# Inverse roots by token: their Newton steps on GpSimd instead of VectorE

## The chip, the cores and the metric

The kernel runs on 1 core of one Trainium2 chip. The metric is the device time of one execution in microseconds (us); lower is better. Before the change it is 2480.51 us, the median of 3 runs (2478.15 to 2484.81).

The engines carry the profile's names: PE (TensorE), DVE (VectorE), ACT (ScalarE), POOL (GpSimd), and SP, which issues most of the DMAs. PSUM is the memory that PE writes its results to, SBUF the working memory of all engines.

## What is computed

Two layers of an encoder trunk for 544 tokens (512 of a prompt and 32 of a sample, which share the weights), model width 1024. Each sub-layer is fed by an RMSNorm and its output is normed again before it is added to the residual h:

```python
def rmsnorm(x, g):
    y = xf * lax.rsqrt(jnp.mean(xf * xf, axis=-1, keepdims=True) + EPS)
    return (y * g.astype(jnp.float32)).astype(x.dtype)

def layer(h, p, ...):
    h = h + FFN_RES * rmsnorm(swiglu(rmsnorm(h, g_ff1_pre), w_ff1_gu, w_ff1_down), g_ff1_post)
    m, state = token_mix(rmsnorm(h, g_mix_pre), ...)          # three kinds of attention
    h = h + rmsnorm(m, g_mix_post)
    h = h + FFN_RES * rmsnorm(swiglu(rmsnorm(h, g_ff2_pre), w_ff2_gu, w_ff2_down), g_ff2_post)
    gate = jax.nn.sigmoid(rmsnorm(h, g_ple_pre) @ w_ple_gate)
    h = h + rmsnorm((p @ w_ple_proj) * gate, g_ple_post)
```

What matters here is the factor `rsqrt(mean(x*x) + EPS)`, one number for each token.

## The kernel before

**Layout.** Activations lie with the feature on the partition and the token on the free axis: h is eight tiles of 128 features by 544 tokens. The tokens are worked in two halves (HALVES): the first has 256 columns, the second 288. Every fp32 operand of a matrix product is split in a high and a low part (`split`, L111: ACT copies the high part, DVE subtracts it from the source, which is recorded as L109 and L113), and `gemm` (L233) makes three matmuls of each block, L238 to L240. A weight block of 128x1024 thus costs a DMA, an ACT copy and a DVE subtraction before PE can use it. The weights arrive through two buffers `raw`.

**The norm by halves.** `Normed` (L245) holds the input of a sub-layer without its root: `chunk` (L255) multiplies h by the gain and splits it (xa, xb; L258, L259) and `square` sums the squares (L205 on ACT, L211 on DVE). The products are made from that, and the root multiplies their result: `up` in `ffn` does `tt(g, pg, x.r(c0, c1))` (L346, L348), `job` in `ple` does it in L973. So PE can run ahead of the root until all six PSUM banks that such products use hold a result that waits for it (three called acc, two prj, one pv). `Finish` (L279) ends a sub-layer: `scale` (L289) makes the root of the output y, `fill` (L297) runs over eight chunks of a half, on DVE z = y * gain * root (L303) and h = h + z (L304), and hands each to the next sub-layer's `chunk`.

**Two ways to the root.** `rstd_wide` (L193) works on the whole 128 x 256 or 128 x 288 tile with Ln and Exp on ACT; the mix (attention) and its entry use it, and the change leaves it alone. `rstd` (L155) works by token: PE adds the squares over the partitions with a matmul against ones (L165, L167), so that the sums of 128 (or 96) tokens stand on as many partitions in 2 (or 3) columns. DVE turns them into v (L171) and a first guess by integer arithmetic (L172, L173), and then runs three Newton steps on the 128x2 or 96x3 tile, three instructions each:

```python
            for _ in range(3):
                tt(e, rc, rc, op=ALU.mult)
                tt(e, e, v, op=ALU.mult)
                stt(rc, e, 1.5, rc, op0=ALU.add, op1=ALU.mult)
```

These are L175, L176 and L177. PE then spreads the root over all partitions with matmuls against the identity (L179, into a tile called tr), and either ACT copies it to SBUF (`copy`, recorded as L109 r<-tr) or DVE reads it from PSUM (L303 with an input tr). `rstd` is called 20 times. Ten places call it, once for each half: the input of the first ffn; in layer 0 the input of the second ffn, its output, the input of ple, the output of ple and the input of the next layer's first ffn; in layer 1 the input of the second ffn, its output, and ple's input and output. In the text they are sites 0 to 19 in order of time, two for each place: sites 2 and 3 (and 12 and 13 in layer 1) are the input of the second ffn, sites 8 and 9 the output of ple in layer 0, 10 and 11 the input of the next ffn, 18 and 19 the output of ple at the program's end.

**What sets the order.** The program is written in the order of the computation, but each engine's instruction order is made by a list scheduler that runs over the whole program with its own estimates of durations and with priorities (`tc.high_priority(300)` around `rstd`). Engines then run their queues strictly in that order and wait on semaphores. A change to one engine's work therefore moves instructions on the others too. DVE's queue mixes the Newton instructions with the fill's and the weight splits; PE's queue holds L179 at the place at which the scheduler expects the root.

POOL has little to do in the kernel: it clears tiles, copies 32x32 blocks (L687) and issues some DMAs, nearly all in the mix.

Of the kernel before, what the change touches and what calls it, by code (L numbers as in the profile page):

```python
# [12 lines left out]
ALU = mybir.AluOpType  # L13
# [22 lines left out]
def trunk(ctx: ExitStack, tc, a, outs, depth=2):  # L36
    nc = tc.nc
# [19 lines left out]
    def tl(tag, shape, dt=F32):  # L57
        count[0] += 1
        tag = alias.get(tag, tag)
        p, n = where[tag]  # L60
        return p.tile(shape, dt, tag=tag, name=f"{tag}_{count[0]}", bufs=n)
# [40 lines left out]
    tt = nc.vector.tensor_tensor  # L102
    stt = nc.vector.scalar_tensor_tensor
# [4 lines left out]
    def copy(out, in_):  # L108
        act(out, in_, AF.Copy)  # L109
# [32 lines left out]
    def load_gains(l):  # L142
# [9 lines left out]
        bfs.append(at.pop("b_f")[0])  # L152
        gains.append(at)

    def rstd(out, acc, n, last=None, rc=None):  # L155


        w = acc.shape[1]
        m = 128 if w % 128 == 0 else 96
        k = w // m  # L160
        with tc.high_priority(300):
            t = bank("tr")
            for i in range(k):
                to, c = t[0:m, 288 + 2 * i:290 + 2 * i], slice(i * m, i * m + m)
                mm(to, acc[:, c], ones[:, 0:2], start=True, stop=last is None)  # L165
                if last is not None:
                    mm(to, last[:, c], ones[:, 0:2], start=False, stop=True)  # L167
            sums = t[0:m, 288:288 + 2 * k].rearrange("p (t two) -> p t two", two=2)[:, :, 0]
            v, e = tl("n", [128, 4])[0:m, 0:k], tl("n", [128, 4])[0:m, 0:k]
            rc = (tl("n", [128, 4]) if rc is None else rc)[0:m, 0:k]  # L170
            ts(v, sums, -0.5 / n, -0.5 * EPS, op0=ALU.mult, op1=ALU.add)  # L171
            ts(rc.bitcast(I32), v.bitcast(I32), 1, MASK, op0=ALU.arith_shift_right, op1=ALU.bitwise_and)  # L172
            ts(rc.bitcast(I32), rc.bitcast(I32), -1, MAGIC, op0=ALU.mult, op1=ALU.add)  # L173
            for _ in range(3):
                tt(e, rc, rc, op=ALU.mult)  # L175
                tt(e, e, v, op=ALU.mult)  # L176
                stt(rc, e, 1.5, rc, op0=ALU.add, op1=ALU.mult)  # L177
            for i in range(k):
                mm(t[:, i * m:i * m + m], rc[:, i:i + 1].to_broadcast([m, 128]), ident[0:m, 0:m], start=True, stop=True)  # L179
            if out is None:  # L180
                return t[:, 0:w]
            copy(out, t[:, 0:w])
# [62 lines left out]
    class Normed:  # L245
# [23 lines left out]
        def r(s, c0, c1):  # L269
            if c0 not in s.done:  # L270
                s.done.add(c0)
                i = c0 // 128
                if s.wide:
                    rstd_wide(s.R[:, c0:c1], s.acc[:, c0:c1], D, tmp="q")
                    return s.R[:, c0:c1]
                rstd(s.R[:, c0:c1], s.acc[:, c0:c1], D, s.last.get(c0), s.rc[:, i:i + 4])
            return s.R[:, c0:c1]

    class Finish:  # L279
# [9 lines left out]
        def scale(s, cols):  # L289
            c0, c1 = cols  # L290
            acc = s.R[c0] = s.acc[:, c0:c1]
            if s.wide:
                rstd_wide(acc, acc, D)
            else:
                s.R[c0] = rstd(None, acc, D, s.last.get(c0))
# [816 lines left out]
def build(nc, shapes, depth=2):  # L1112
    from concourse import mybir as _m
    import numpy as np
    args = {k: nc.dram_tensor(f"in_{k}_dram", s, _m.dt.float32, kind="ExternalInput").ap() for k, s in shapes.items()}
    outs = [nc.dram_tensor(f"out_{i}_dram", s, _m.dt.float32, kind="ExternalOutput").ap()
            for i, s in enumerate(_outputs(depth))]
    with tile.TileContext(nc, schedule_with_timeline_sim=True) as tc:
        trunk(tc, args, outs, depth)
    return len(outs)  # L1120
# [13 lines left out]
```

## Time and profile before

| | |
|---|---|
| median of 3 runs | 2480.51 us |
| profiled execution, its own time | 2481.84 us |
| its span, first to last instruction | 2480.0 us |
| PE busy (matmuls) | 2390.8 us, 96% |
| DVE busy | 1443.3 us, 58% |
| ACT busy | 1083.7 us, 44% |
| POOL busy | 71.7 us, 3% |
| TensorE clock granted, mean | 0.981 |

Durations are read from the one profiled execution. A wait is time in which an engine's next instruction was held back, and it is put down to the instruction that released it. Times in a timeline count from the start of the span.

### The profile page before, as it was taken

What the parts mean: (1) busy time and instruction counts of PE and PEld (TensorE: products, weight loads), DVE (VectorE), ACT (ScalarE), POOL (GpSimd) and SP (SyncE); (2) the same over time, 40 slices, a digit from 0 to 9 for tenths busy, and PEclk for the clock granted to TensorE, in tenths of its full rate; (3) what the DMA queues carried; (4) which work ended last, traced back from release to release, by engine and by line L of the source; (5) the groups of instructions that cost most, each with busy time, mean ns of one, the idle gap of its engine ahead of it and who ended that gap; (6) DMA issues with size and microseconds to landing.
All of it is one profiled execution on the core that took longest, in us unless ns stands there. A gap on an engine that the chain in (4) does not pass through costs nothing.

```text
span 2480.0 us, 45319 instructions
## 1 busy us (share of the span) xinstructions
PE 2390.8 (96%) x18342; PEld 2302.4 (93%) x18342; DVE 1443.3 (58%) x3236; ACT 1083.7 (44%) x2347; POOL 71.7 (3%) x244
## 2 busy tenths in 40 slices
PE   9999999999998999999999999999999989999997
PEld 8999999987788999999999999999876889999997
DVE  6344446777857344446863444477777573444466
ACT  5322224668854322224533222246788543222343
POOL 0000000211000000000000000001110000000000
PEclk9999999999998999999999999999999999999998
DMA  5323322322023323322213323232311233323221
GB/s 161 108 79 90 100 66 82 95 89 55 27 65 115 111 80 90 99 86 86 82 47 98 98 72 106 56 97 91 101 33 34 77 111 98 95 74 102 85 69 37
DMA packets 73600, 207.44 MB, mean 84 GB/s; under 512 B 9312, under 2 KB 18152, under 8 KB 73392
## 3 DMA queue, kind: packets, MB, share of 16 engines
q1 hardware_dynamic: 70288, 195.93, 26.5%
q0 software_dynamic: 3104, 8.62, 1.1%
q8 instruction: 144, 2.36, 0.4%
q14 instruction: 64, 0.52, 0.1%
HBM read 188.21 MB, written 11.85 MB: 81 GB/s over the span
## 4 chain that ended last, share of the span: by engine, by line
PE 88%; DVE 6%; ACT 3%; DMA 2%; issue 1%; SPq 0%; DVEq 0%; ACTq 0%
PE acc L238 12%; PE acc L239 12%; PE acc L240 12%; PE prj L238 10%; PE prj L239 10%; PE prj L240 10%; PE pv L238 4%; PE pv L239 4%; PE pv L240 4%; PE acc L405 2%; PE tr L135 1%; DMA raw<-in_w_ff_gu_dram 1%; DVE z L303 1%; PE pv L427 1%; PE pv L429 1%; PE pv L428 1%
## 5 line engine op out<-in xcount | busy, mean ns | idle before, releaser
L109 ACT ACTIVATE wx<-raw 128x1024 fp32r<-128x1024 f32 (+3 forms) x149 | 139.3, 936 | 269.8 <-PE acc L239 99.4
L109 ACT ACTIVATE wh<-raw 128x1024 fp32r<-128x1024 f32 (+3 forms) x157 | 151.2, 966 | 228.9 <-PE acc L239 101.9
L113 DVE TENSOR_TENSOR wl<-raw,wh 128x1024 fp32r<-128x1024 f32 (+3 forms) x157 | 173.6, 1107 | 80.8 <-ACT wh L109 80.0
L109 ACT ACTIVATE m<-q 128x256 fp32r<-128x256 f32 (+1 forms) x224 | 94.9, 428 | 256.9 <-DVE q L349 251.9
L113 DVE TENSOR_TENSOR wx<-raw,wx 128x1024 fp32r<-128x1024 f32 (+3 forms) x149 | 159.4, 1070 | 77.8 <-ACT wx L109 75.8
L238 PE MATMUL prj<-xa,wh 128*128 128x256 f32 (+3 forms) x632 | 186.4, 295 | 4.6 <-DVE q L346 2.7
L239 PE MATMUL prj<-xb,wh 128*128 128x256 f32 (+3 forms) x632 | 186.2, 295 | 4.5 <-DVE xb L259 4.5
L240 PE MATMUL prj<-xa,wl 128*128 128x256 f32 (+3 forms) x632 | 184.5, 292 | 0.0
L238 PE MATMUL acc<-xa,wx 128*128 128x256 f32 (+1 forms) x600 | 173.9, 290 | 5.4 <-ACT wx L109 5.4
L240 PE MATMUL acc<-xa,wx 128*128 128x256 f32 (+1 forms) x600 | 173.9, 290 | 0.0
L239 PE MATMUL acc<-xb,wx 128*128 128x256 f32 (+1 forms) x600 | 173.6, 289 | 0.0
L239 PE MATMUL acc<-xb,wh 128*128 128x288 f32 (+1 forms) x576 | 166.7, 290 | 0.0
L240 PE MATMUL acc<-xa,wl 128*128 128x288 f32 (+1 forms) x576 | 166.5, 290 | 0.0
L238 PE MATMUL acc<-xa,wh 128*128 128x288 f32 (+1 forms) x576 | 165.6, 290 | 0.0
L240 PE MATMUL prj<-xa,wx 128*128 128x288 f32 (+1 forms) x480 | 139.8, 291 | 1.3 <-DVE wx L113 1.3
L238 PE MATMUL prj<-xa,wx 128*128 128x288 f32 (+1 forms) x480 | 140.4, 293 | 0.0
L239 PE MATMUL prj<-xb,wx 128*128 128x288 f32 (+1 forms) x480 | 140.3, 292 | 0.0
L347 ACT ACTIVATE q<-q 128x256 f32<-128x256 f32 (+1 forms) x176 | 74.3, 425 | 145.6 <-DVE q L346 141.2
L239 PEld LDWEIGHTS prj<-xb,wh 128*128 128x128 f32 (+1 forms) x632 | 119.6, 189 | 7.1 <-DVE xb L259 6.2
L238 PEld LDWEIGHTS prj<-xa,wh 128*128 128x128 f32 (+1 forms) x632 | 119.4, 189 | 7.3 <-DVE q L346 3.2
L240 PE MATMUL acc<-xa,wy 128*128 128x288 f32 (+1 forms) x424 | 123.4, 291 | 0.8 <-DVE wy L113 0.8
L238 PE MATMUL acc<-xa,wy 128*128 128x288 f32 (+1 forms) x424 | 123.7, 292 | 0.4 <-ACT wy L109 0.4
(525 smaller groups left out, 8128.2 us busy)
## 6 DMA issues: line engine op xcount, KB each, us to landing
raw<-in_w_ff_gu_dram SPq DMA_DIRECT2D x174, 512.0 KB, 3.6
raw<-in_w_ff_down_dram SPq DMA_DIRECT2D x64, 384.0 KB, 3.2
raw<-in_w_ff_down_dram SPq DMA_DIRECT2D x64, 320.0 KB, 2.9
raw<-in_w_in_dram SPq DMA_DIRECT2D x22, 512.0 KB, 3.5
raw<-in_w_out_dram SPq DMA_DIRECT2D x16, 512.0 KB, 3.6
raw<-in_w_ple_gate_dram SPq DMA_DIRECT2D x16, 512.0 KB, 3.5
raw<-in_w_v_dram SPq DMA_DIRECT2D x8, 512.0 KB, 3.6
xb<-r SPq DMA_DIRECT2D x32, 128.0 KB, 2.3
```

Of the source, the lines that this page charges most:

```text
L109: act(out, in_, AF.Copy)
L113: tt(lo, src, f(hi), op=ALU.subtract)
L135: nc.tensor.transpose(out, in_, ident[0:n, 0:n])
L238: mm(p, wh[k], xh[k][:, c0:c1], start=i == 0, stop=False)
L239: mm(p, wh[k], xl[k][:, c0:c1], start=False, stop=False)
L240: mm(p, wl[k], xh[k][:, c0:c1], start=False, stop=i == len(ks) - 1)
L303: stt(t, s.y[c][:, c0:c1], s.g[c], s.R[c0], op0=ALU.mult, op1=ALU.mult)
L347: act(g, g, AF.Silu)
L405: one = mm(ss[e][:, 0:w], z[a_][:, qs], z[b_][:, 0:w], start=(a_, b_) == (0, 2), stop=False)
L427: mm(Oe, vh, ph[:, j, :], start=e == 0 and j == 0, stop=False, skip_group_check=True)
L428: mm(Oe, vl, ph[:, j, :], start=False, stop=False, skip_group_check=True)
L429: mm(Oe, vh, pl[:, j, :], start=False, stop=j == 2 * b + 1, skip_group_check=True)
```

## The change

The three-instruction Newton step goes from DVE to POOL, where it takes four instructions, since the fused add and multiply is split in two. v, the integer guess, the matmuls and the copies stay where they are, and so does `rstd_wide`.

```diff
+    ptt, pts = nc.gpsimd.tensor_tensor, nc.gpsimd.tensor_scalar
+
     def rstd(out, acc, n, last=None, rc=None):
...
             ts(rc.bitcast(I32), v.bitcast(I32), 1, MASK, op0=ALU.arith_shift_right, op1=ALU.bitwise_and)
             ts(rc.bitcast(I32), rc.bitcast(I32), -1, MAGIC, op0=ALU.mult, op1=ALU.add)
             for _ in range(3):
-                tt(e, rc, rc, op=ALU.mult)
-                tt(e, e, v, op=ALU.mult)
-                stt(rc, e, 1.5, rc, op0=ALU.add, op1=ALU.mult)
+                ptt(e, rc, rc, op=ALU.mult)
+                ptt(e, e, v, op=ALU.mult)
+                pts(e, e, 1.5, None, op0=ALU.add)
+                ptt(rc, rc, e, op=ALU.mult)
             for i in range(k):
                 mm(t[:, i * m:i * m + m], rc[:, i:i + 1].to_broadcast([m, 128]), ident[0:m, 0:m], start=True, stop=True)
```

The lines behind it move down by three: L179 is L182 in the changed kernel, L303 is L306, L346 is L349. In the program, 180 instructions leave DVE's queue and 240 enter POOL's, and the scheduler orders the queues anew; PE and ACT have as many instructions as before.

POOL's queue at its head, in the changed kernel (n is the tile of v or e, rc that of the root; ISA is an instruction that the compiler puts in):

```order
L397 MEMSET pa_5189 128x128
L397 MEMSET pa_5190 128x128
L177 ISA
L177 TENSOR_TENSOR n_300<-rc_124 128x2
L178 TENSOR_TENSOR n_300<-n_300,n_299 128x2
L179 TENSOR_SCALAR n_300<-n_300 128x2
L180 TENSOR_TENSOR rc_124<-rc_124,n_300 128x2
L177 TENSOR_TENSOR n_300<-rc_124 128x2
```

Site 0's chain stands right behind the first two clears, with an ISA row ahead of it that stands nowhere else in front of such a chain; each link but the first waits for the one before it.

PE's queue at site 2, the input of the second ffn of layer 0 (acc, prj and pv are the six banks, wh and wl a weight's two parts), before:

```order
L238 MATMUL acc_9408<-xa_9035,wh_9401 128x256
L239 MATMUL acc_9408<-xb_9043,wh_9401 128x256
L240 MATMUL acc_9408<-xa_9035,wl_9402 128x256
L179 MATMUL tr_9293<-cst,rc_9046 128x128 x2
L238 MATMUL prj_9479<-xa_9028,wh_9467 128x256
```

and in the changed kernel:

```order
L241 MATMUL acc_9417<-xa_9038,wh_9410 128x256
L242 MATMUL acc_9417<-xb_9046,wh_9410 128x256
L182 MATMUL tr_9299<-cst,rc_9052 128x128 x2
L243 MATMUL acc_9417<-xa_9038,wl_9411 128x256
L241 MATMUL acc_9417<-xa_9039,wh_9410 128x256
L242 MATMUL acc_9417<-xb_9047,wh_9410 128x256
```

The spreading matmuls have moved up by ten matmuls, from behind the sixth bank's last product into the middle of that product. Behind them the first product that needs a freed bank is prj, in both.

DVE's queue at the same site, where the root is first used (L346 and L348, in the changed kernel L349 and L351), before:

```order
L211 TENSOR_TENSOR r_9044<-r_9044,z_9170 128x288
L304 TENSOR_TENSOR y_8734<-t_9175,z_9173 128x288
L177 SCALAR_TENSOR_TENSOR rc_9046<-n_9299,rc_9046 128x2
L303 SCALAR_TENSOR_TENSOR z_9183<-y_8770,gt_77,r_8500 128x288
L259 SCALAR_TENSOR_TENSOR xb_9040<-y_8734,gt_77,xa_9032 128x288
L304 TENSOR_TENSOR y_8770<-t_9185,z_9183 128x288
L211 TENSOR_TENSOR r_9044<-r_9044,z_9180 128x288
L303 SCALAR_TENSOR_TENSOR z_9193<-y_8806,gt_77,r_8500 128x288
L346 TENSOR_TENSOR q_9291<-prj_9241,r_9045 128x256
L348 TENSOR_TENSOR q_9292<-pv_9242,r_9045 128x256
```

and in the changed kernel:

```order
L214 TENSOR_TENSOR r_9050<-r_9050,z_9156 128x288
L307 TENSOR_TENSOR y_8639<-t_9161,z_9159 128x288
L113 TENSOR_TENSOR wx_9483<-raw_9480,wx_9482 128x1024
L349 TENSOR_TENSOR q_9297<-prj_9247,r_9051 128x256
L351 TENSOR_TENSOR q_9298<-pv_9248,r_9051 128x256
L349 TENSOR_TENSOR q_9394<-acc_9344,r_9051 128x256
L306 SCALAR_TENSOR_TENSOR z_9169<-y_8704,gt_77,r_8506 128x288
```

The use of the root has moved up past two chunks of the fill and one weight split: it stands behind the fill's third chunk and the split of the fourth weight.

## Rows read from the trace of the kernel before

**Rows 1.** The page: busy time, then the chain that ended last.
```profile
PE 2390.8 (96%) x18342; PEld 2302.4 (93%) x18342; DVE 1443.3 (58%) x3236; ACT 1083.7 (44%) x2347; POOL 71.7 (3%) x244
PE 88%; DVE 6%; ACT 3%; DMA 2%; issue 1%; SPq 0%; DVEq 0%; ACTq 0%
```

**Rows 2.** Waits of PE: waiting line, releaser, us in total, times, longest.
```profile
PE tr L179 <- DVE rc L177: 17.3, 3, 7.3
PE tr L179 <- DVE n L177: 3.0, 2, 2.4
```

**Rows 3.** Stretches: length, busy us (count) by engine, PEclk, DMA share, GB/s.
```profile
755.00:790.00 35.00, 26.39 (x193) 25.89 (x193) 29.06 (x79) 17.59 (x34) 0.00 (x0) 0.80 0.31 97
790.00:1145.00 355.00, 355.00 (x2834) 355.00 (x2833) 161.94 (x280) 107.65 (x178) 0.00 (x0) 1.00 0.31 92
```

**Rows 4.** Timeline of PE at sites 2, 12, 10, 19: start, us, instruction [idle before].
```profile
764.18 0.28 PE L240 MATMUL acc<-xa,wl 128*128 128x256 f32 x1
771.73 1.22 PE L179 MATMUL tr<-cst,rc 128*128 128x128 f32 x4 [7.28 <-DVE rc L177]
774.28 0.58 PE L238 MATMUL prj<-xa,wh 128*128 128x256 f32 x1 [1.33 <-DVE q L346]
...
775.09 0.41 PE L238 MATMUL prj<-xa,wh 128*128 128x256 f32 x1
775.30 0.41 PE L239 MATMUL prj<-xb,wh 128*128 128x256 f32 x1
...
2005.51 0.58 PE L238 MATMUL prj<-xa,wh 128*128 128x256 f32 x1 [1.32 <-DVE q L346]
...
1256.81 0.71 PE L179 MATMUL tr<-cst,rc 128*128 128x128 f32 x4 [3.08 <-DVE rc L177]
...
2468.69 1.59 PE L179 MATMUL tr<-cst,n 96*128 96x96 f32 x6 [2.38 <-DVE n L177]
```

**Rows 5.** Timeline of DVE at site 2, from the guess to the root's use.
```profile
757.66 0.16 DVE L173 TENSOR_SCALAR rc<-rc 128x2 int32<-128x2 int32 x1
758.15 0.15 DVE L175 TENSOR_TENSOR n<-rc 128x2 f32<-128x2 f32 x1
758.84 1.23 DVE L113 TENSOR_TENSOR wl<-raw,wh 128x1024 fp32r<-128x1024 f32 x1 [0.53 <-ACT wh L109]
759.98 0.94 DVE L303 SCALAR_TENSOR_TENSOR z<-y,gt,r 128x288 f32<-128x288 f32 x2
...
765.84 1.23 DVE L113 TENSOR_TENSOR wx<-raw,wx 128x1024 fp32r<-128x1024 f32 x1 [0.73 <-ACT wx L109]
...
771.52 0.15 DVE L177 SCALAR_TENSOR_TENSOR rc<-n,rc 128x2 f32<-128x2 f32 x1
...
773.81 0.42 DVE L346 TENSOR_TENSOR q<-prj,r 128x256 f32<-128x256 f32 x1
```

**Rows 6.** Timeline of DVE at site 19: first and last of nine.
```profile
2466.95 0.16 DVE L175 TENSOR_TENSOR n<-n 96x3 f32<-96x3 f32 x1
...
2468.48 0.16 DVE L177 SCALAR_TENSOR_TENSOR n<-n,n 96x3 f32<-96x3 f32 x1
```

**Rows 7.** Timeline of POOL in the mix: copies of 32x32, then two dependent clears.
```profile
486.95 0.49 POOL L687 COPY s<-kl 32x32 f32<-32x32 f32 x1 [3.63 <-DVE kl L677]
487.48 0.42 POOL L687 COPY s<-kl 32x32 f32<-32x32 f32 x1
487.94 0.20 POOL L687 COPY s<-kl 32x32 f32<-32x32 f32 x1
412.43 0.40 POOL L747 MEMSET st<- 36x288 f32 x2 [3.41 <-issue]
412.88 0.33 POOL L747 MEMSET st<- 4x288 f32 x1
```

**Rows 8.** Timeline of DVE beside those copies.
```profile
486.95 0.43 DVE L211 TENSOR_TENSOR r<-r,sq 128x256 f32<-128x256 f32 x1
487.35 0.48 DVE L638 SCALAR_TENSOR_TENSOR m<-q,gt,m 128x256 fp32r<-128x256 f32 x1
```

## The prediction

> **What bounds the kernel now.** I read the page first. PE is busy 96% of the span and carries 88% of the chain that ended last, DVE is at 58% and POOL at 3% [rows 1]. So the time is PE's own work, plus PE's waits, plus what it loses at the lower clock. POOL is free to take work, and DVE's work costs something only where PE waits for it.
>
> The list of PE's waits says where that is. The spreading matmuls L179 wait for the last Newton instruction L177 five times, 17.3 + 3.0 = 20.3 us in all [rows 2]. That is what a quicker root can win; the other 15 of the 20 calls make PE wait nowhere.
>
> The stretches tell what such a wait lies in. Around site 2 DVE is busy 29.06 of 35 us and PE only 26.39, at a mean clock of 0.80; in the 355 us after it PE never pauses, 2834 matmuls in 355 us, 0.125 us each [rows 3]. In that steady part nothing is waited for, so whatever PE gains or loses at a site stays.
>
> The timelines show the mechanism. At site 2 PE has filled its six banks at about 764.4, then waits 7.28 us for the root, spreads it, and waits 1.33 us more until DVE's L346 frees a bank at 774.28 [rows 4]. On DVE the guess is ready at 757.82, and nine Newton instructions of 0.15 us need until 771.67, because the fill and the weight splits stand between them [rows 5]. The arithmetic is small; the place in DVE's queue is what costs.
>
> **The change, part by part.**
>
> *A link on POOL.* No row shows a two-input instruction of POOL on so small a tile. The nearest is the copy of 32x32, 0.20 us where nothing disturbs it, and between two clears of which the second waits for the first lie 0.05 us (412.83 to 412.88) [rows 7]. So a link costs 0.25 at least. At most I set 0.55: the longest copy, 0.49, and a gap. I take 0.30, near the undisturbed copy with something for the second operand. Twelve links are then 3.6 us, against nine DVE instructions in 2466.95 to 2468.64, 1.7 us, where DVE does nothing else [rows 6]. Undisturbed, POOL is slower by 1.9.
>
> *Beside a busy DVE.* The copies of 0.49 and 0.42 us end at 487.44 and 487.90, 0.07 us behind the ends of the two DVE instructions beside them, 487.38 and 487.83; both of these read two operands from SBUF [rows 7, 8]. So a link that meets such an instruction waits for its end. L113, L303, L304, L259 and L211 are of that kind when their inputs are in SBUF. While DVE runs them back to back, one link passes at each boundary: 0.4 to 0.5 us for fill instructions (0.94 for two), 1.2 us for a split [rows 5].
>
> *Sites 2 and 12.* From 757.9 three links fit before the split at 758.84, the fourth ends with it at 760.1, four more pass between four fill instructions (761.8), one with the next split (763.0), and three with fill instructions: about 764.3, not 771.67. The new order puts 66 large matmuls between the last sum and L182, which PE ends at about 763.0 (764.4 less the ten now behind L182 [rows 4]), so PE still waits 1.4 us there. But the bank comes free only when DVE reaches L349, which now stands behind the split of 765.84, so at about 767.0, and PE goes on at about 767.5 instead of 774.28: **-6.8 us**. Site 12 repeats the pattern and ends in the same 1.32 us wait for L346 [rows 4]: again -6.8, in all **-13.6**. After the wait PE ran 24 matmuls at the lower clock, 0.21 apart instead of 0.125 [rows 3, 4], about 2 us a site. If the wait shrinks to some 3 us in two pieces, the clock may or may not fall; I take half, **-2** for both, between 0 and -4.
>
> *Sites 8 to 11.* The 3.0 us of the waits for tile n are 2.38 at site 19 and 0.6 at site 8, which goes: **-0.6** [rows 2, 4]. At site 10 PE waits 3.08 us for a chain spaced out by the fill as at site 2 [rows 4]. It ends earlier, but the new order also has PE there earlier; I take -2, and -1 for the low clock after it: **-3**, between 0 and -7.
>
> *The other 15 sites, 19 apart.* There PE now gets to the spreading matmuls late enough. The scheduler moved them up: 40 to 69 large matmuls lie between sums and L182, 50 at most sites, or 6.3 us [rows 3]. The root needs about 1.1 us for v, the guess and the handing over, and then 3.6 us of links alone or 5 to 6 beside the fill. So it is between 1.6 us early and 0.8 late; site 0, with 42 matmuls, is the tightest. I take 0.3 us of new wait at each of these 14: **+4.2**, between 0 and +11.
>
> *Site 19.* Nothing covers it: PE waits 2.38 us and DVE is idle behind it [rows 4, 6]. 3.6 + 0.1 for the second handing over, less 1.7: **+2.0**, between +1.4 and +5.
>
> *At no cost.* POOL has nothing else to do at these sites, and its clears and DMAs lie in the mix, so nothing is queued behind a chain [rows 1]. DVE loses 180 x 0.155 = 28 us of work; its worth is in the terms above.
>
> *A rule against it.* As the copies show it, POOL waits for DVE; the DVE instruction that began while a copy was waiting took 0.48 us, no longer than its fill-sized kin (0.94 for two) [rows 5, 8]. The Trainium skill, SBUF — State Buffer, section "Who interferes with whom", says that it goes by issue order: whichever of the two engines starts first holds the shared ports for its whole instruction, and the other is blocked fully. By that DVE too would wait, which is the third rival.
>
> **Sum.** -13.6 - 2 - 0.6 - 3 + 4.2 + 2.0 = -13.0 us. The sum is made against the profiled execution, 2481.84 us (span 2480.0), which lies 1.3 us above the median of 2480.51: 2468.8 by the one, 2467.5 by the other. I say **2468**. A measurement of this kernel tells about 0.3% from no change, 7.4 us: faster is below 2473, slower above 2488.
>
> **Rivals.**
>
> 1. *The time is given back.* PE runs ahead by 7 us at site 2 and meets the next limit, the fill of the second half, with DVE at 29 of 35 us [rows 3]. For it: the new order puts six products' reads (L349, L351) ahead of that fill. Against it: PE is given products of the second half chunk by chunk, so that it need not wait for the last. If half of the 15.6 us at sites 2 and 12 goes, -5: 2476. Chance 16%.
>
> 2. *Slower: the link.* If a two-input link costs more than about 0.5 us, every root comes late, as PE's queue now stands on the scheduler's earlier time. At 0.6: 1.1 + 7.2 - 6.3 = 2.0 us late at 14 sites, +28, and +5.6 at site 19, against gains of 19: 2496. It breaks even near 0.52. For it speaks the copy of 0.49 us; against it that this one ended with DVE's instruction and the free one took 0.20 [rows 7, 8]. 13%.
>
> 3. *DVE waits for POOL.* If each link holds DVE for its 0.2 us, a site costs DVE 2.4 us; where DVE sets PE's pace (2, 10, 12) that is +7: 2475. Against it stands the unchanged 0.48 us [rows 8]. 7%.
>
> 4. *The new ISA row.* It stands ahead of site 0's chain, and no row of the trace has its price. The chain is wanted at about 15.8 us and POOL is free from about 1, so up to 14 us are hidden; at 25 us PE would stand still for some 8: 2476. 4%. The Trainium skill, GPSIMD Engine Reference, section "Instruction dispatch", names about 6 us for the first call to freshly loaded code; by that it costs nothing.
>
> **How the numbers follow.** My forecast has 60%, its own range 2457 to 2475: from all new waits away, full clock and -7 at site 10, to new waits near 0.7 us a site. Rivals 1, 3 and 4 are no change, and so is a small piece of the forecast: 0.29. Faster keeps 0.58, slower is rival 2, 0.13. The range from 2456 to 2482 takes in rivals 1, 3 and 4 and leaves out rival 2 and a little below.
>
> **What would show it.** In the changed profile: POOL with 240 more instructions, links of 0.2 to 0.3 us, longer beside DVE instructions with two SBUF operands and ending with them; at sites 2 and 12 the root 7 us earlier, and PE's wait before prj ended by L349 at about 767.5; PE's waits for POOL many and short; site 19 2 us longer. I am wrong if links are above 0.5 us, if PE's waits for POOL sum to over 20 us, or if sites 2 and 12 keep their 8 us.

## The result, and the profile after

The changed kernel takes **2464.81 us**, the median of 4 runs (2463.59 to 2466.10), beside 2481.66 us for the kernel before on the same chip. The ratio is **0.9929**, 95% interval 0.9917 to 0.9941: faster by 0.7%, some 17 us. The forecast was 2468, the range 2456 to 2482. The profiled execution took 2463.9 us, its span is 2462.0, the mean granted clock 0.987 (before 0.981).

The page's busy times and the engines' shares of the chain that ended last, against [rows 1]:

```profile
PE 2383.6 (97%) x18342; PEld 2293.6 (93%) x18342; DVE 1421.9 (58%) x3056; ACT 1080.9 (44%) x2347; POOL 154.0 (6%) x484
PE 86%; DVE 6%; ACT 3%; DMA 2%; POOL 1%; issue 1%; SPq 0%; DVEq 0%; POOLq 0%; ACTq 0%
```

POOL has the 240 instructions more and 82 us of work more, DVE 180 fewer and 21 us less. The span is 18.0 us shorter. PE, with the same matmuls, is busy 7.2 us less, so it idled 10.8 us less, and ran for less time at the lower of its two clocks (1.2 instead of 2.4 GHz): 2462 x 2 x (1 - 0.987) = 64 us where the kernel before has 2480 x 2 x (1 - 0.981) = 94.

PE's waits for the root (line, releaser, us in total, times, longest), against [rows 2]:

```profile
PE tr L182 <- POOL rc L180: 8.0, 6, 2.7
...
PE tr L182 <- POOL n L180: 4.9, 1, 4.9
```

20.3 us became 12.9: two waits of 7 went, small ones came, and the one of site 19 grew from 2.4 to 4.9. The stretches of [rows 3]:

```profile
755.00:790.00 35.00, 32.74 (x267) 32.33 (x266) 28.26 (x66) 18.78 (x37) 6.69 (x15) 1.00 0.38 118
790.00:1145.00 355.00, 355.00 (x2836) 355.00 (x2835) 165.21 (x288) 110.08 (x182) 3.47 (x12) 1.00 0.31 92
```

At site 2 PE does 267 matmuls in the 35 us instead of 193, at a granted clock of 1.00 instead of 0.80, and DVE is nearly as busy as before (28.26 instead of 29.06 us). Behind it PE again never pauses, so what was won there stays won. The timeline of PE at sites 2, 12, 0, 10 and 19, against [rows 4]:

```profile
766.45 0.28 PE L242 MATMUL acc<-xb,wh 128*128 128x256 f32 x1
768.42 0.71 PE L182 MATMUL tr<-cst,rc 128*128 128x128 f32 x4 [1.69 <-POOL rc L180]
...
770.88 0.39 PE L241 MATMUL prj<-xa,wh 128*128 128x256 f32 x1 [0.57 <-DVE q L349]
...
1986.22 0.71 PE L182 MATMUL tr<-cst,rc 128*128 128x128 f32 x4 [1.62 <-POOL rc L180]
...
22.46 0.71 PE L182 MATMUL tr<-cst,rc 128*128 128x128 f32 x4 [0.90 <-POOL rc L180]
...
1247.48 1.02 PE L182 MATMUL tr<-cst,rc 128*128 128x128 f32 x4 [2.70 <-POOL rc L180]
...
2450.72 1.59 PE L182 MATMUL tr<-cst,n 96*128 96x96 f32 x6 [4.86 <-POOL n L180]
```

At site 12 the clock stays up as well, 0.57 before and 1.00 after:

```profile
1998.00:2010.00 12.00, 5.71 (x29) 5.42 (x30) 11.52 (x32) 7.00 (x14) 0.00 (x0) 0.57 0.27 82
1984.00:1996.00 12.00, 10.38 (x86) 10.17 (x85) 11.87 (x29) 7.71 (x16) 1.92 (x4) 1.00 0.55 164
```

Now the chain itself. POOL at site 2, eight of its twelve links:

```profile
761.29 0.38 POOL L177 TENSOR_TENSOR n<-rc 128x2 f32<-128x2 f32 x1 [81.75 <-DVE rc L175]
761.75 1.19 POOL L178 TENSOR_TENSOR n<-n,n 128x2 f32<-128x2 f32 x1
763.03 0.37 POOL L179 TENSOR_SCALAR n<-n 128x2 f32<-128x2 f32 x1
...
764.62 0.22 POOL L179 TENSOR_SCALAR n<-n 128x2 f32<-128x2 f32 x1
764.92 1.11 POOL L180 TENSOR_TENSOR rc<-rc,n 128x2 f32<-128x2 f32 x1
766.12 0.35 POOL L177 TENSOR_TENSOR n<-rc 128x2 f32<-128x2 f32 x1
...
766.99 1.10 POOL L179 TENSOR_SCALAR n<-n 128x2 f32<-128x2 f32 x1
768.17 0.19 POOL L180 TENSOR_TENSOR rc<-rc,n 128x2 f32<-128x2 f32 x1
```

and DVE beside it:

```profile
761.66 1.23 DVE L113 TENSOR_TENSOR wl<-raw,wh 128x1024 fp32r<-128x1024 f32 x1
...
764.76 1.23 DVE L113 TENSOR_TENSOR wl<-raw,wh 128x1024 fp32r<-128x1024 f32 x1 [0.28 <-ACT wh L109]
...
766.33 0.94 DVE L262 SCALAR_TENSOR_TENSOR xb<-y,gt,xa 128x288 fp32r<-128x288 f32 x2
767.19 0.45 DVE L214 TENSOR_TENSOR r<-r,z 128x288 f32<-128x288 f32 x1
767.56 0.45 DVE L307 TENSOR_TENSOR y<-t,z 128x288 f32<-128x288 f32 x1
```

The links of 1.19 and 1.11 us end at 762.94 and 766.03, 0.05 and 0.04 behind the two splits. The twelve take 7.07 us here. At site 19, where DVE is idle, they take 3.27:

```profile
2447.39 0.19 POOL L177 TENSOR_TENSOR n<-n 96x3 f32<-96x3 f32 x1 [9.95 <-DVE n L175]
2447.66 0.19 POOL L178 TENSOR_TENSOR n<-n,n 96x3 f32<-96x3 f32 x1
2447.93 0.22 POOL L179 TENSOR_SCALAR n<-n 96x3 f32<-96x3 f32 x1
...
2450.47 0.19 POOL L180 TENSOR_TENSOR n<-n,n 96x3 f32<-96x3 f32 x1
```

So a link costs 0.27 us undisturbed (0.19, or 0.22 for the one with a constant, and 0.08 to the next). From the first link's start to the last one's end the 20 chains take 5.0 us on average.

**Where the time went.** The table lines up the same matmul (by its number on PE) in two traces and says by how much the later kernel gained (-) or lost (+) on the kernel before in each part of the program. The experiments below have their columns here too.

| us against the kernel before | changed | e1 | e2 | e3 | e9 | e4 | e5 | e6 | e7 | e8 |
|---|---|---|---|---|---|---|---|---|---|---|
| start, sites 0 and 1 | +1.4 | +1.1 | +1.9 | +0.1 | +0.3 | +5.2 | +1.9 | +0.3 | +3.4 | -0.6 |
| to the end of the first mix | +1.7 | +0.5 | +1.8 | +2.2 | +2.8 | +0.5 | +0.8 | +0.3 | +1.2 | +1.9 |
| sites 2 and 3 | -9.1 | -8.2 | +0.3 | -3.0 | -5.8 | -1.8 | -8.2 | -7.9 | -9.6 | -9.8 |
| sites 4 to 6 | -0.6 | +3.0 | -0.6 | 0.0 | -0.4 | +3.8 | -0.5 | -0.2 | -0.2 | -0.2 |
| sites 7 to 11 | -4.5 | +1.8 | -5.8 | -3.5 | -0.1 | +5.0 | -4.5 | -3.1 | -8.7 | -8.4 |
| to the end of the second mix | +0.8 | +3.4 | -3.2 | -2.6 | -0.2 | +2.9 | -2.9 | +1.0 | -4.1 | +1.7 |
| sites 12 and 13 | -8.9 | -8.7 | -0.6 | -4.2 | -4.8 | -0.4 | -8.8 | -8.7 | -9.5 | -9.1 |
| sites 14 to 17 | -0.4 | -0.5 | -0.4 | -0.2 | -0.6 | +4.6 | -0.9 | -0.5 | +0.1 | 0.0 |
| sites 18 and 19 | +1.5 | -0.3 | +1.7 | 0.0 | -0.2 | +5.9 | +1.7 | 0.0 | +0.8 | -0.2 |
| sum | -18.0 | -7.9 | -4.9 | -11.3 | -8.8 | +25.7 | -21.4 | -18.9 | -26.6 | -24.7 |

How much of a row is an effect? No edit touches the mix, but the scheduler may order it anew. In the first mix all the queues stand in the same order in all these traces (only 2 instructions moved in e4 and 37 in e9). In the second they do not: in the changed kernel, e1, e4 and e6 some 260 to 350 of PE's 4516 matmuls between 1320 and 1940 us stand in another order than in the kernel before, in e3, e5, e7, e8 and e9 a few tens of instructions. Where nothing at all was moved two executions still differ. In the second mix e2 has every queue of the kernel before and is 3.2 us quicker; e7 and e8 have each other's queues and lie 5.8 us apart, at a granted clock of 0.99 and 0.98. At sites 7 to 11 the changed kernel, e2 and e6 have the same queues and gain 4.5, 5.8 and 3.1. So a single row tells little below some 3 us, in the second mix below some 6.

### The profile page after: what moved, and what is told of

The parts are those of the page before. It is cut to its first block, busy times and chain, and to the rows that moved or that the text cites. A ratio compares the mean times of both kernels' runs of the same rounds, so it can differ in the third digit from the quotient of the medians.

```text
span 2462.0 us, 45413 instructions
## 1 busy us (share of the span) xinstructions
PE 2383.6 (97%) x18342; PEld 2293.6 (93%) x18342; DVE 1421.9 (58%) x3056; ACT 1080.9 (44%) x2347; POOL 154.0 (6%) x484
## 4 chain that ended last, share of the span: by engine, by line
PE 86%; DVE 6%; ACT 3%; DMA 2%; POOL 1%; issue 1%; SPq 0%; DVEq 0%; POOLq 0%; ACTq 0%
PE acc L242 12%; PE acc L241 12%; PE acc L243 12%; PE prj L241 10%; PE prj L242 10%; PE prj L243 10%; PE pv L241 4%; PE pv L242 4%; PE pv L243 4%; PE acc L408 2%; PE tr L135 1%; DMA raw<-in_w_ff_gu_dram 1%; DVE z L306 1%; PE pv L432 1%; PE pv L430 1%
## 5 line engine op out<-in xcount | busy, mean ns | idle before, releaser
L242 PE MATMUL acc<-xb,wy 128*128 128x288 f32 (+1 forms) x424 | 123.5, 291 | 0.0
```

The lines of the kernel that those rows point to most:

```text
L242: mm(p, wh[k], xl[k][:, c0:c1], start=False, stop=False)
```

## The experiments

Theory: the gain comes where the chain stood in DVE's queue between fill instructions and splits (sites 2 and 12, less so 8 to 11), because the root comes earlier. Rivals: DVE simply has less to do; or the order in DVE's queue is all, and POOL is not needed. And the second rival of the prediction, the price of a link, wants a number.

**e1 and e2: where the gain is.** A counter of the calls picks the engine; e1 takes POOL at four sites, e2 at the other sixteen.

```diff
+            site[0] += 1
             for _ in range(3):
-                ptt(e, rc, rc, op=ALU.mult)
...
+                if site[0] in (2, 3, 12, 13):
+                    ptt(e, rc, rc, op=ALU.mult)
...
+                else:
+                    tt(e, rc, rc, op=ALU.mult)
```

In e2 the condition is `site[0] not in (2, 3, 12, 13)`.

> Newton steps on POOL at the input of the second ffn alone (sites 2, 3, 12, 13), on DVE at the other sixteen. Theory (the gain comes from sites 2 and 12, where the chain stood in DVE's queue between fill instructions and splits): both sites keep the changed kernel's waits, about 2 us instead of 8 each, and the clock does not fall behind them; time before minus 15 to 18 us, so about 2464 to 2467, with PE's waits at the other sites as before the change (0.6 us at site 8, 3.1 at site 10, 2.4 at site 19). Rival (the gain is spread over all sites, because DVE has 28 us less to do): about a fifth of the gain, four sites of twenty, so 2478.

> The complement: POOL at sixteen sites, DVE at sites 2, 3, 12, 13. Theory: sites 2 and 12 keep their 8 us of wait; sites 8 to 11 give 2 to 5 us, site 0 costs 1, site 19 costs 1.5 to 2.5; time before minus 0 to 3 us, 2478 to 2482. Rival (relief of DVE counts everywhere): four fifths of the gain, about 2468.

e1: 2472.69 us, ratio 0.9957 (0.9944 to 0.9971). e2: 2477.73 us, ratio 0.9982 (0.9972 to 0.9991). Neither is where the theory put it. The two reductions, 0.43% and 0.18%, add up to 0.61%, near the whole change's 0.71% (each is known to about 0.1%), so no large help or hindrance between the parts shows. By the table the theory holds for the sites themselves: e1 wins 8.2 and 8.7 us at 2, 3, 12 and 13, and e2 keeps the old waits there:

```profile
PE tr L190 <- DVE rc L188: 13.7, 2, 7.3
```

But e2 also wins 5.8 us at sites 7 to 11, more than the 2 to 5 expected, and e1 loses 8.7 us in parts that it doesn't touch (sites 4 to 11 and the two mixes). Part of that is the clock. In the stretch around sites 4 and 5, where all its queues stand in the order of the kernel before, e1 has a granted clock of 0.83:

```profile
1150.00:1170.00 20.00, 18.54 (x129) 18.25 (x128) 16.02 (x45) 10.86 (x26) 0.00 (x0) 0.83 0.33 104
```

and the kernel before and the changed one have 1.00 in the same stretch:

```profile
1150.00:1170.00 20.00, 18.48 (x149) 18.19 (x148) 17.40 (x47) 12.13 (x25) 0.00 (x0) 1.00 0.51 158
1150.00:1170.00 20.00, 19.12 (x158) 18.71 (x157) 16.62 (x40) 12.13 (x28) 3.23 (x12) 1.00 0.35 107
```

PE waited 0.69 and 0.76 us in e1 ahead of that, 0.33 and 1.18 in the kernel before, 0.17 and 0.71 in the changed kernel. Why the clock fell in one and not in the others stays open. In the second mix e1's queues stand in an order of their own, and there PE idles 21.2 us instead of 18.4.

**e3 and e9: the chain on DVE, but earlier in its queue.** e3 is the kernel before with this at the end of `run_jobs` (`link[0]` is the chain's last instruction; `issue_after` orders instructions of one engine):

```diff
-        if fin:
+        if fin and fin.nx and fin.wide and not fin.to_mix:
+            fin.nx.r(*HALVES[0])
+            with tc.issue_after(link[0].ins):
+                fin.fill(HALVES[1])
+        elif fin:
             fin.fill(HALVES[1])
```

> No POOL at all: the kernel before, with the root of the first half asked for ahead of the fill of the second half at sites 2 and 12, and that fill's DVE instructions queued behind the chain's last one. If the place in DVE's queue was what cost (theory), nine instructions of 0.15 us with a split or two of 1.2 between them end some 4 to 5 us after v instead of 14, PE waits under 1.5 us there, and the time is that of the changed kernel or up to 5 us better at these sites: 2460 to 2467. If the work on DVE was what cost (rival: the fill is the bound, so it pays later what the chain gained), PE waits for the fill instead and the time is 2474 to 2482.

2470.74 us, ratio 0.9951 (0.9936 to 0.9966): between the two. The wait for the root is gone altogether, more so than with POOL, but PE then stands in front of the next thing. PE's longest total wait in e3 (L352 is L346 of the kernel before):

```profile
PE prj L240 <- DVE q L352: 10.7, 2, 5.8
```

The root was spread at 767.18. ACT copied it to SBUF only at 771.14, behind two copies of weights of which the first waited for its DMA:

```profile
767.72 1.06 ACT L109 ACTIVATE wx<-raw 128x1024 fp32r<-128x1024 f32 x1 [3.21 <-DMA raw<-in_w_ff_gu_dram]
...
770.20 1.04 ACT L109 ACTIVATE wx<-raw 128x1024 fp32r<-128x1024 f32 x1
771.14 0.36 ACT L109 ACTIVATE r<-tr 128x256 f32<-128x256 f32 x1
```

and on DVE the read that frees the bank stood behind their splits:

```profile
768.80 1.23 DVE L113 TENSOR_TENSOR wx<-raw,wx 128x1024 fp32r<-128x1024 f32 x1 [0.98 <-ACT wx L109]
...
771.97 1.22 DVE L113 TENSOR_TENSOR wx<-raw,wx 128x1024 fp32r<-128x1024 f32 x1
773.11 0.41 DVE L352 TENSOR_TENSOR q<-prj,r 128x256 f32<-128x256 f32 x1
```

In the changed kernel the same copy comes at 769.17 and the read at 770.41. So the change did two things at these sites: the root came earlier, and the scheduler moved the reads up on DVE; e3 has the first without the second. e9 therefore also moves the splits of later weights behind the reads:

```diff
+            if qi == 0 and before_last:
+                for k in range(3):
+                    up(k, *HALVES[0])
+                with tc.issue_after(link[1].ins):
+                    up(3, *HALVES[0])
+                    for k in range(4):
+                        up(k, *HALVES[1])
...
```

(`link[1]` is the last read so far, the second line in `up` that uses `x.r`.)

> e3 (no POOL, chain ahead of the second half's fill on DVE) took the wait for the root away at sites 2 and 12, but PE then waited 5.79 and 4.88 us for the read that frees its first bank, which stood on DVE behind two weight splits. Here the splits of the fourth and later weights are queued behind the sixth such read as well. Theory (the place in the queues is what costs, POOL is only one way to mend it): PE's wait for the bank falls to 1 to 2 us, perhaps with 1 us for a split that is now late, each site gives 3 to 4 us more than in e3, and the time is that of the changed kernel within 3 us: 2462 to 2467. Rival (DVE cannot carry the chain and the fill in this stretch, whatever the order): the wait goes to a late split or to the fill, 2469 to 2475.

2469.39 us, ratio 0.9945 (0.9930 to 0.9961), with a wide scatter (2463.43 to 2476.80 in 7 runs; the trace is of a run of 2472.97). The wait for the bank fell, to 3.32 us at site 2 and 2.92 at site 12, not to 1 or 2:

```profile
772.09 0.39 PE L240 MATMUL prj<-xa,wh 128*128 128x256 f32 x1 [3.32 <-DVE q L352]
```

No split stands ahead of the read any more. What is left is on ACT:

```profile
768.08 1.06 ACT L109 ACTIVATE wx<-raw 128x1024 fp32r<-128x1024 f32 x1 [2.51 <-DMA raw<-in_w_ff_gu_dram]
...
770.55 0.36 ACT L109 ACTIVATE r<-tr 128x256 f32<-128x256 f32 x1
```

So neither theory nor rival is settled in full. The order alone, with no instruction on POOL, gives 10.6 us at sites 2, 3, 12 and 13 where the changed kernel has 18.0, and the rest of the wait goes from queue to queue (root, then DVE's splits, then ACT's copy). Whether a third mending, on ACT, would bring DVE level with POOL wasn't tried.

**e4: a link of twice the price.** `range(3)` becomes `range(6)` in the changed kernel.

> The changed kernel with six Newton steps instead of three, so 24 links: as long as twelve links of about 0.55 us, just above the break-even of 0.52 that the second rival of the prediction names. By the prediction's sum every one of the 14 ordinary sites is then some 1.4 us late (+20), sites 2, 12, 10 and 19 lose 3 to 5 each (+12 to +20): 2485 to 2505. Rival (the scheduler moves the spreading matmuls back as far as the chain grows, and the slack of 0.5 to 2 us at most sites takes the rest): only sites 2, 12 and 19 lose, 2470 to 2478.

2509.96 us, ratio 1.0113 (1.0094 to 1.0133): 27 us slower than the kernel before and 5 above the upper end. PE's waits for the root:

```profile
PE tr L182 <- POOL rc L180: 22.6, 7, 6.3
PE tr L182 <- POOL n L180: 18.7, 8, 9.5
```

They go from 12.9 to 41.3 us. Ten of the 15 sites at which the kernel before didn't wait now do, 13.4 us together; with twelve links three of them waited, 2.0 us. The scheduler did move the spreading matmuls back, at most sites by 25 to 30 matmuls or some 3.4 us, but not as far as the chain grew. The expectation had taken the links at their undisturbed 0.27 us, 6.5 us for 24. Beside DVE's instructions the 20 chains took 6.7 to 12.8 us, 9.8 on average (twelve links: 5.0). Even so the waits grew by 28.4 us only, less than the 32 to 40 that the expectation adds up. What puts the time above its upper end is PE's pace: by the pages the same matmuls keep PE busy for 2399.0 us instead of 2383.6, 15.4 more, at a mean granted clock of 0.979 instead of 0.987. The mechanism of the second rival is real, and the clock adds half as much again.

**e5: DVE as busy as before.** Nine DVE instructions of the old kind, chained, whose result nobody reads:

```diff
+            d = tl("n", [128, 4])[0:m, 0:k]
...
+            for i in range(3):
+                tt(d, v, v if i == 0 else d, op=ALU.mult)
+                tt(d, d, v, op=ALU.mult)
+                stt(d, d, 1.5, v, op0=ALU.add, op1=ALU.mult)
```

> The changed kernel, and beside each POOL chain nine more DVE instructions of the size and order of the old Newton steps, chained to each other and asked for with the same priority, whose result nobody reads. DVE is as busy as before the change (28 us more than now), but the root does not wait for it. Theory (what counts is that the root no longer passes through DVE's queue): sites 2 and 12 keep their short waits, 2463 to 2469. Rival (what counts is that DVE has less to do there): the gain at 2, 12 and 8 to 11 goes back by half or more, 2473 to 2482.

2461.38 us, ratio 0.9917 (0.9902 to 0.9933): not slower at all. DVE has its 3236 instructions again, and PE's wait at site 2 is 1.21 us:

```profile
767.55 0.71 PE L187 MATMUL tr<-cst,rc 128*128 128x128 f32 x4 [1.21 <-POOL rc L181]
```

That DVE has less to do (21 us by the pages, not the 28 that 180 x 0.155 gives; e5 puts 18 back) is worth nothing here. What counts is that the root does not wait in its queue. (The 3 us under the changed kernel can't be told from scatter: by the table they come in the second mix, where e5's queues are also nearly those of the kernel before and not the changed kernel's.)

**e6, e7, e8: what is left.** e6 puts sites 0, 1, 18 and 19 back on DVE (`if 1 < site[0] < 18` for POOL). e7 reaches the same precision with ten links, and e8 does both.

```diff
-            for _ in range(3):
-                ptt(e, rc, rc, op=ALU.mult)
...
+            ptt(e, rc, rc, op=ALU.mult)
+            ptt(e, e, v, op=ALU.mult)
+            pts(p, e, 1.5, 2.5, op0=ALU.mult, op1=ALU.add)
+            ptt(e, e, p, op=ALU.mult)
+            pts(e, e, 1.875, None, op0=ALU.add)
+            ptt(rc, rc, e, op=ALU.mult)
...
```

(A Newton step of four links follows.)

> The changed kernel with the Newton steps of sites 0, 1, 18 and 19 back on DVE, where no fill or little of it stands between them. Theory (nothing covers POOL's longer chain there): site 0 gives back the wait of 0.9 us, site 19 2.5 of its 4.85, the rest is unchanged: 3 to 4 us under the changed kernel, 2461. Rival (the clock at the end is low anyway and the first matmuls wait for weights): under 1.5 us, 2463.5 to 2465.

> The changed kernel with ten POOL links instead of twelve to the same precision: one third-order step of six instructions and one Newton step of four in place of three Newton steps. Undisturbed a link takes 0.27 us, so 0.54 less; beside DVE some 1.2 less. Theory (PE waits for POOL at sites 0, 2, 6, 10, 12, 16 and 19, so each gives the links' time): 0.5 each, more at 2 and 12, in all 3 to 5 us under the changed kernel: 2460 to 2462. Rival (the scheduler moves the spreading matmuls up by as much, three to five of them, and at 2 and 12 the bank's read comes next anyway): only site 19 gives 0.5: 2464.

> The two before together: ten links on POOL at sites 2 to 17, nine DVE instructions at 0, 1, 18 and 19. If both theories hold the gains add: 6 to 7 us under the changed kernel, 2458. If both rivals hold: 2463. It would be the quickest version of these either way.

e6: 2463.31 us, ratio 0.9926 (0.9914 to 0.9939). The waits went as expected (none at site 0, 2.77 at site 19), which is 1.1 and 1.5 us in the table, but sites 2 and 3 and sites 7 to 11, with the same queues as the changed kernel, gave 1.2 and 1.4 less, and the times can't be told apart. e7: **2456.69 us**, ratio 0.9900 (0.9886 to 0.9913), below the interval of the changed kernel and better than either expectation. At site 10 the wait is 0.60 instead of 2.70 us:

```profile
1247.39 0.71 PE L188 MATMUL tr<-cst,rc 128*128 128x128 f32 x4 [0.60 <-POOL rc L186]
```

and the clock stays up there, 1.00 in e7

```profile
1235.00:1275.00 40.00, 37.69 (x303) 37.20 (x302) 27.21 (x70) 17.20 (x40) 10.77 (x29) 1.00 0.11 34
```

where the changed kernel has 0.91:

```profile
1235.00:1275.00 40.00, 36.37 (x273) 35.87 (x272) 23.05 (x60) 14.30 (x32) 10.69 (x32) 0.91 0.06 18
```

That is 4 of the 8.6 us in the table, and e8 shows it again (-8.4 there). Another 5 lie in the second mix; e8, with the same queues there, has none of them, so part of the 8 us between the medians may be scatter. At the start e7 loses 2 us (a new wait of 2.07 at site 1). e8 mends that, 2458.07 us, ratio 0.9903 (0.9889 to 0.9916), the same as e7 within their intervals, and the 2458 that was expected: by the table 3.7 us come at both ends and 3.9 at sites 7 to 11. Both beat both kernels.

## Why the prediction was right

Direction and mechanism were right and the time lies within the range. The gain in the traces was 5 us larger than the sum of -13.0, because PE's pace gave more and the new waits cost less than I took; one of the terms that fit did so by luck (sites 8 to 11).

| term | forecast | traces |
|---|---|---|
| sites 2 and 12, waits | -13.6 | -12.8 |
| low clock behind them | -2, 0 to -4 | -5.2 |
| sites 8 to 11 | -3.6: waits -2.6, low clock -1 | -4.5 (7 to 11): waits -1.4, the rest -3.1 |
| other sites | +4.2, 0 to +11 | +0.4 |
| site 19 | +2.0 | +1.5 |
| the mix | none | +2.5 |
| sum | -13.0 | -18.0 |

*A link.* 0.30 was taken between 0.25 and 0.55; it is 0.27 undisturbed (the gap is 0.08 where the two clears had 0.05). That a link which meets a DVE instruction with two operands in SBUF ends just behind it was right: all 24 links above 0.9 us end 0.04 to 0.10 us behind such an instruction. That one passes at each boundary was too simple. The link of 766.99 let the boundaries at 767.19 and 767.56 go by and ended only behind L307.

*Sites 2 and 12.* The forecast had the chain take 6.4 us from the guess (it took 7.1), a wait of 1.4 for the root (1.69 and 1.62), and then the read L349 as the next limit. The waits for the root and the bank went from 8.61 to 2.26 us at site 2 and from 8.31 to 1.62 at site 12. With the short waits for weights around them, which changed little, PE idles 6.1 us less at sites 2 and 3 and 6.7 less at 12 and 13: 12.8 us of 13.6. PE goes on at 770.88; the trace reaches the site 3.1 us late (start and mix, in the table above), so in the time of [rows 4] that is 767.8, for the 767.5 of the forecast.

*The low clock* was undersized. I took half of 2 us a site, not knowing whether it would fall. It did not fall at either site, and the parts of the gain there that are no waits are 3.0 and 2.2 us, more than the 2 a site even in full. The forecast had counted the matmuls behind the waits and not the spreading ones, which went from 1.22 us to 0.71. The mean clock between 755 and 790 went from 0.80 to 1.00, at site 12 from 0.57 to 1.00. That this remainder is the clock's is read from the rows; no run holds the wait and changes the clock alone.

*Sites 8 to 11.* The wait of site 8 went as forecast. At site 10 PE's wait was to fall by 2 us and fell by 0.4, from 3.08 to 2.70: the chain, beside the fill, still takes 5.9 us there. What made up for it is PE's pace. The granted clock is 0.91 in the changed kernel's row of 1235 to 1275 above; the kernel before has 0.87 at the same place:

```profile
1245.00:1285.00 40.00, 35.95 (x255) 35.59 (x255) 27.16 (x82) 15.62 (x34) 0.00 (x0) 0.87 0.09 26
```

With the same queues e2 gains 5.8 us and e6 3.1 in this part, so that the sum of -3.6 came near was luck.

*The other sites* were the step that failed: +4.2 us of new waits, 0.3 at each of 14 (beside 2, 8, 10, 12 and 19 there are 15, a slip that changes little). Three of them wait, 0.90 (site 0, named as the tightest), 0.55 and 0.55; twelve don't. The estimate put the root between 1.6 us early and 0.8 late and then took a wait at each; what measured it is e4, where ten wait with chains 4.8 us longer. PE's queue has slack, and I had counted none. *Site 19* waits 2.5 us more where 2.0 was worked out, 1.6 of them for the longer chain; 1.5 reach the end.

*The rivals.* (1) Nothing is given back: PE never pauses from 790 to 1145. (2) Links were cheap enough: in place, DVE's instructions included, the 20 chains take 3.3 to 7.1 us, 5.0 on average, or 0.42 a link. In e4 they take 9.8 on average. Between -18.0 us at 5.0 and +25.7 at 9.8 a straight line crosses zero near 7.0, or 0.58 for each of twelve links; that is drawn from two points, but the break-even of 0.52 was of the right size. (3) DVE does not wait: its split takes as long as before. The groups of the kernel before,

```profile
L113 DVE TENSOR_TENSOR wl<-raw,wh 128x1024 fp32r<-128x1024 f32 x105 | 128.5, 1223 | 70.1 <-ACT wh L109 69.4
L304 DVE TENSOR_TENSOR h<-h,z 128x288 f32<-128x288 f32 x24 | 10.4, 453 | 0.0
```

and of the changed kernel:

```profile
L113 DVE TENSOR_TENSOR wl<-raw,wh 128x1024 fp32r<-128x1024 f32 x105 | 128.3, 1223 | 74.5 <-ACT wh L109 74.1
L307 DVE TENSOR_TENSOR h<-h,z 128x288 f32<-128x288 f32 x24 | 10.4, 453 | 0.0
```

The 17 splits of 128x1024 that began while a link was under way took 1.227 us on average, the 224 beside which there was none 1.224. The rule of the Trainium skill (SBUF — State Buffer, section "Who interferes with whom"), that whichever of the two starts first blocks the other, agrees with these traces in one direction only: DVE's instruction held POOL for its whole length, and no row shows a link of 0.19 us holding DVE. (4) The new ISA row cost nothing that the trace shows; the first link stood ready when the guess came, and took 0.39 us:

```profile
16.16 0.39 POOL L177 TENSOR_TENSOR n<-rc 128x2 f32<-128x2 f32 x1 [15.09 <-DVE rc L175]
```

## What to carry to other kernels

A chain of tiny dependent instructions is priced by what stands between its links in its engine's queue, not by its busy time: look at how long the waiting engine stands, and move the chain to a queue that is empty, even if each link is slower there. Taking work off an engine that is not the bound gained nothing by itself (e5). When such a wait goes, read the next one in the same place before you count the gain (the bank's read on DVE, the copy on ACT), and count the links on the new engine: they are cheap only as long as PE's queue has slack for them (e4, e7).

## What the runs showed that was not expected

- POOL does not slip in at every boundary of back-to-back DVE instructions: beside a run of fill instructions a link of 0.2 us took up to 1.2.
- PE's waits of 0.69 and 0.76 us were followed by a granted clock of 0.83 in e1, and those of 0.33 and 1.18 by 1.00 in the kernel before, in the same stretch with the same queues. Between traces whose queues don't differ there, the second mix thus differs by up to 5.8 us, as much as some of the effects looked for.
- An edit at a few sites makes the scheduler order the second mix anew, hundreds of us away. In e1 PE idles 2.8 us more there.
- Two links fewer of twelve gave 8 us between the medians, part of it perhaps scatter, where the waits for POOL sum to 12.9 and fell by 2.8 alone: at site 10, in e7 and in e8, a wait of some 0.6 in place of 2.70 came with a clock that stayed up.
